# Up products 352 wide, with 32 tokens' inner values gathered early and written into the gate matrix as weights

## The chip, the core and the metric

The kernel runs on one core of a Trainium2 chip. The measure is the device time of one execution in microseconds. A core has five engines with instruction streams of their own: TensorE (PE in the profile, with its weight loads as PEld), VectorE (DVE), ScalarE (ACT), GpSimd (POOL) and SyncE (SP). Each of them works in the order of its own stream; they wait for one another by semaphores. DMAs are issued from the streams of SP, ACT and POOL.

## The reference, cut to what matters

A trunk of two layers over 512 tokens, 1024 wide. In each layer three causal mixers (attention, a short convolution, gated linear attention) are followed by a PEER channel mixer: a product-key lookup chooses, for each token, 8 heads x 16 of 16384 experts, each of them one row of u and one of v.

```python
def peer(xn, w_q, keys1, keys2, u, v):
    ...
    s1 = jnp.einsum('thd,nd->thn', q[:, :, 0], keys1).astype(jnp.float32)
    s2 = jnp.einsum('thd,nd->thn', q[:, :, 1], keys2).astype(jnp.float32)
    v1, i1 = lax.top_k(s1, PEER_TOPK)
    v2, i2 = lax.top_k(s2, PEER_TOPK)
    cand = (v1[..., :, None] + v2[..., None, :]).reshape(T, PEER_HEADS, PEER_TOPK * PEER_TOPK)
    sc, ci = lax.top_k(cand, PEER_TOPK)
    ...
    experts = (e1 * PEER_NKEYS + e2).reshape(T, hk)
    gates = jax.nn.softmax(sc, axis=-1).reshape(T, hk).astype(xn.dtype)
    ...
    def block(args):
        xb, eb, gb = args
        ub = jnp.take(u, eb, axis=0)
        hb = jax.nn.gelu(jnp.einsum('tkd,td->tk', ub, xb), approximate=False)
        vb = jnp.take(v, eb, axis=0)
        return jnp.einsum('tk,tkd->td', gb * hb, vb)
```

So for a token the output is the sum over its 128 chosen experts of gate x gelu(u row . x) x v row.

## The kernel before

**Two ways to the same sum.** For the first TD = 368 tokens PEER is computed densely, over all 16384 experts in 128 chunks of 128. `hidden` forms the inner values of a chunk (expert by token) as the up product of u and x, with GELU by ACT on the way out of PSUM (tile psh to tile ht). A gate matrix G, which is zero where a token has not chosen an expert, is multiplied in (`weigh`), and `accumulate` forms the down product with v into six PSUM banks (pv), 384 tokens by 1024. The last 128 tokens (block 3 of 4) and the 16 that remain of block 2 (tokens 368 to 383) go by gathering: an indirect DMA on POOL's queue fetches for each of the 128 partitions the row of one chosen expert, a DVE operation forms the inner product with x (`inner`, with accumulation along the row) or adds the weighted row of v to a sum (`outer`, into yacc).

**Three bf16-like parts.** Every large product is done in three matmuls (`mm3`) from a high and a low part of each operand; ACT makes the high part (a cast), DVE the low part (a subtraction). So each chunk of u, of v and of the weighted inner values costs an ACT and a DVE operation.

**The stages of the PEER part of a layer.** First the queries and the best keys of each head (`best`). Then the *up stage*: NPRE = 72 chunks, whose inner values are stored to memory (H), and three more; beside them DVE works at the routing (`routing`): for each block of 128 tokens `route` finds the 16 best of the candidates of each head, with their expert indices and gates, and `gate_matrix` builds G for 16 tokens at a time. For that it makes one-hot matrices of both halves of the expert index (oha, ohb) on DVE, multiplies one of them by the gate's high and low parts in fp16 (ohh, ohl), and PE multiplies 128x128 one-hots (psg) whose sums ACT copies out and stores. Then the *mixed stage*: 56 chunks in which an up product (24 matmuls, 368 columns) and a down product (18 matmuls, 512 columns) take turns. Then the *down stage*: 72 chunks of down products alone, with inner values that come back from H. The last three chunks' down products are prepared ahead (`ahead_v`, `ahead_hi`, `ahead_lo`) and stand at the end, one block of tokens at a time, with the next layer's norm between them.

**What sets the order.** The program is written in order; instructions marked `pin` stay in that order on their engine, the others are placed by a scheduler between them. Two generators run beside the chunks. `routing` is paced by DVE_STEP: it gives back the DVE time that it thinks it used, and gets 2.72 us of it a chunk. `gathered`, the row gathers, is paced by `tick` and RATE: 0.8 rows a chunk in the up stage (once the routing of block 3 is done), 3.3 in the mixed and 1.12 in the down stage. ROUTE_AT = 1 sets the routing of block 3 behind that of block 0.

**The 16 tokens between.** `route` of block 2 stores their experts and gates to memory (xidx, xgat); in the mixed stage, between the v rows of block 3, `spread` loads them so that the 16 tokens x 128 experts lie as 128 partitions x 16 (with the token's x repeated, tile xg), gathers 16 rows of u, then 16 of v, and a matmul with a placing matrix (psx) adds the eight partial sums of a token together and puts them at the tokens' rows.

**Buffers.** Four split chunks of u (tags uwa, uwb; NUW), five gathered rows (seven once the routing has closed), four raw v chunks, two tiles of G.

Of the kernel before, what the change touches and what calls it, by code (L numbers as in the profile page):

```python
# [19 lines left out]
P = 128  # L20
# [10 lines left out]
TD = 368  # L31
# [6 lines left out]
NPRE = 72  # L38
# [11 lines left out]
RATE = (0.8, 3.3, 1.12)  # L50
DVE_STEP = 2.72
ROUTE_AT = 1
# [20 lines left out]
class K:  # L73
# [18 lines left out]
    def setup(self):  # L92
# [10 lines left out]
        self.xidx = self.dr.tile([NX, P], I32, tag="xidx", name="xidx")  # L103
        self.xgat = self.dr.tile([NX, P], F32, tag="xgat", name="xgat")
# [623 lines left out]
    def peer(self, L, xh, xl, rest):  # L728
        nc, tc, ins = self.nc, self.tc, self.ins
        G = self.dr.tile([NCH // GE, P, TD // TBAT, GE * TBAT], F32, tag="G", name="G")  # L730
        H = self.dr.tile([NPRE, P, TD], F32, tag="H", name="H")
        with ExitStack() as pc:
# [9 lines left out]
            def new_h():  # L742
                if len(hts) < NHT:
                    hts.insert(0, self.up.tile([P, TW], F32, name=f"ht{len(hts)}", bufs=1))
                    nc.gpsimd.memset(hts[0][:, TD:TW], 0.0)
                else:
                    hts.insert(0, hts.pop())
# [70 lines left out]
            for j in range(NQ):  # L818
# [4 lines left out]
                if j == 3:  # L823
                    pin(nc.sync.dma_start(xg, ins["norm_ffn"][L:L + 1, :].partition_broadcast(P)))
# [12 lines left out]
                if j == 4:  # L837
                    nc.vector.scalar_tensor_tensor(xg, self.x[:, 3], self.rs3, xg, op0=OP.mult, op1=OP.mult)
# [33 lines left out]
            def spread():  # L872
                dma = nc.gpsimd.dma_start
                for _ in range(8):
                    yield False
                for i in range(NX):
                    dma(xg[i * XS:(i + 1) * XS], self.xrows[i:i + 1, :].partition_broadcast(XS))
                dma(xix, self.xidx.rearrange("i (s k) -> (i s) k", k=XR))
                dma(gat[:, 0:XR], self.xgat.rearrange("i (s k) -> (i s) k", k=XR))
                for _ in range(8):  # L880
                    yield False
                for k in range(XR):
                    inner(xix[:, k:k + 1], hd[:, k:k + 1])
                    yield True
                nc.scalar.activation(hd[:, 0:XR], hd[:, 0:XR], AF.Gelu)
                nc.vector.tensor_tensor(hd[:, 0:XR], hd[:, 0:XR], gat[:, 0:XR], op=OP.mult)
                for _ in range(8):
                    yield False
                dma(gat, ins["c_place"])
                for k in range(XR):  # L890
                    outer(xix[:, k:k + 1], hd[:, k:k + 1], xg, k == 0)
                    yield True
                for half in range(2):
# [468 lines left out]
```

## Time and profile before

| | |
|---|---|
| median of 3 runs | 2927.74 us (2927.54 to 2932.99) |
| the profiled execution, its own time | 2929.99 us |
| its span, first to last instruction | 2928.2 us |
| mean granted clock of TensorE | 0.999 |
| PE busy / weight loads busy | 2898.9 us / 2576.4 us |
| DVE / ACT / POOL busy | 2448.1 / 1254.0 / 858.8 us |
| moved by DMA | 788.65 MB, mean 269 GB/s |

The profile shows one execution. A row of a group gives the line, the engine, the operation, the tile written and those read, the count, the busy time, the mean of one in ns, and the engine's idle time ahead of it with what ended it. A row of the timeline gives the start and the length in us; in brackets the idle time ahead of it. A row of stretches gives, for a window in us, its length and then the busy time of the engines in the order of its heading. Matmuls overlap: each shows longer than the distance to the next one.

### The profile page before, as it was taken

The page shows a single profiled execution, that of the slowest core. Times are in us where ns is not written, and L with a number is a line of the kernel's source. Part 1 is how long each engine was busy: PE and PEld are TensorE (multiplying, and loading weights), DVE is VectorE, ACT ScalarE, POOL GpSimd, SP SyncE. Part 2 cuts the span into 40 slices and gives each one's busy share as a digit, 9 for nine tenths or more (in the row PEclk, how much of TensorE's full clock was granted, in tenths as well). Part 3 has the DMA queues.
Part 4 walks back from the last instruction along what each step waited for, and adds up shares of the span by engine and source line. Part 5 has one row for each costly group of instructions (what it writes and reads, how often), then busy time and mean ns, then how long its engine had stood idle before and what let it go on. Part 6 is the DMA issues. An engine that isn't in the chain of part 4 may idle for free.

```text
span 2928.2 us, 44773 instructions
## 1 busy us (share of the span) xinstructions
PE 2898.9 (99%) x16206; PEld 2576.4 (88%) x16206; DVE 2448.1 (84%) x4828; ACT 1254.0 (43%) x1910; POOL 858.8 (29%) x735
## 2 busy tenths in 40 slices
PE   8999999999999999999999999999999999999998
PEld 7878899999999998788888788999999999988887
DVE  6675998996888898988966769999958888988888
ACT  6253355655333332333453533556653333323333
POOL 1200001221555665322112000012215556663221
PEclk9999999999999999999999999999999999999999
DMA  4322258999999999999633222689989999999995
GB/s 130 94 69 82 88 171 269 314 303 352 335 362 359 348 395 349 393 361 370 261 97 90 68 82 88 205 272 314 314 319 354 370 366 347 394 347 386 370 373 210
DMA packets 342334, 788.65 MB, mean 269 GB/s; under 512 B 32640, under 2 KB 189344, under 8 KB 338016
## 3 DMA queue, kind: packets, MB, share of 16 engines
q1 hardware_dynamic: 160624, 430.73, 40.8%
q0 software_dynamic: 86400, 306.56, 28.5%
q10 hardware_dynamic: 95088, 48.50, 5.5%
q8 instruction: 127, 2.08, 0.3%
q14 instruction: 95, 0.78, 0.1%
HBM read 704.64 MB, written 77.89 MB: 267 GB/s over the span
## 4 chain that ended last, share of the span: by engine, by line
PE 85%; DVE 6%; issue 3%; DMA 3%; ACT 2%; POOL 1%; SPq 0%; DVEq 0%; ACTq 0%; POOLq 0%
PE pv L85 10%; PE psh L86 10%; PE psh L84 10%; PE pv L86 10%; PE psh L85 10%; PE pv L84 10%; PE psp L86 2%; PE psp L85 2%; PE psp L84 2%; PE psq L84 2%; PE psq L85 2%; PE psq L86 2%; PE psg L1290 1%; PE psg L1291 1%; DMA row<-in_v_rows,idx 1%
## 5 line engine op out<-in xcount | busy, mean ns | idle before, releaser
L857 POOL DMA_INDIRECT row<-in_u_rows,idx x256 | 371.4, 1451 | 989.2 <-DVE idx L1243 457.7
L85 PE MATMUL pv<-vl,wh 128*128 128x512 f32 x1500 | 582.9, 391 | 0.4
L86 PE MATMUL pv<-vh,wl 128*128 128x512 f32 x1500 | 582.4, 391 | 0.0
L84 PE MATMUL pv<-vh,wh 128*128 128x512 f32 x1500 | 575.0, 390 | 0.0
L857 POOL DMA_INDIRECT row<-in_v_rows,idx x256 | 326.6, 1276 | 431.9 <-DVE yacc L870 343.3
L774 ACT ACTIVATE ht<-psh 128x368 f32<-128x368 f32 x256 | 122.5, 478 | 733.3 <-PE psh L86 716.9
L1001 DVE TENSOR_TENSOR vl<-vraw,vh 128x1024 fp32r<-128x1024 f32 x250 | 305.6, 1223 | 83.5 <-ACT vh L1006 73.5
L863 DVE SCALAR_TENSOR_TENSOR row<-row,xg 128x1024 f32<-128x1024 f32 x288 | 345.5, 1219 | 0.0
L84 PE MATMUL psh<-ahi,uwb 128*128 128x368 f32 x1024 | 340.4, 332 | 0.0
L84 PE MATMUL psh<-ahi,uwa 128*128 128x368 f32 x1024 | 339.9, 332 | 0.0
L86 PE MATMUL psh<-ahi,uwa 128*128 128x368 f32 x1024 | 339.5, 332 | 0.0
L86 PE MATMUL psh<-ahi,uwb 128*128 128x368 f32 x1024 | 339.4, 331 | 0.0
L85 PE MATMUL psh<-alo,uwb 128*128 128x368 f32 x1024 | 337.7, 330 | 0.0
L85 PE MATMUL psh<-alo,uwa 128*128 128x368 f32 x1024 | 337.5, 330 | 0.0
L870 DVE SCALAR_TENSOR_TENSOR yacc<-row,wk,yacc 128x1024 f32<-128x1024 f32 x254 | 325.1, 1280 | 11.4 <-DMA row<-in_v_rows,idx 10.2
L86 PEld LDWEIGHTS pv<-vh,wl 128*128 128x128 f32 x1500 | 281.1, 188 | 60.5 <-DVE wl L1001 1.5
L85 PEld LDWEIGHTS pv<-vl,wh 128*128 128x128 f32 x1500 | 280.9, 188 | 59.9 <-DVE vl L1001 2.9
L84 PEld LDWEIGHTS pv<-vh,wh 128*128 128x128 f32 x1500 | 281.5, 188 | 56.1 <-ACT wh L1014 0.5
L1014 ACT CAST wh<-ht 128x384 fp32r<-128x384 f32 x250 | 128.0, 512 | 444.4 <-DVE ht L1166 405.5
L1006 ACT CAST vh<-vraw 128x1024 fp32r<-128x1024 f32 x250 | 262.4, 1050 | 1.4 <-PE pv L85 1.4
L759 DVE TENSOR_TENSOR uwb<-uraw,uwb 128x1024 fp32r<-128x1024 f32 x144 | 175.9, 1221 | 103.7 <-ACT uwb L758 97.2
L759 DVE TENSOR_TENSOR uwa<-uraw,uwa 128x1024 fp32r<-128x1024 f32 x144 | 175.3, 1221 | 71.8 <-ACT uwa L758 68.6
(381 smaller groups left out, 5828.0 us busy)
## 6 DMA issues: line engine op xcount, KB each, us to landing
uraw<-in_peer_u SPq DMA_DIRECT2D x256, 512.0 KB
vraw<-in_v_rows SPq DMA_DIRECT2D x256, 512.0 KB
G<-stg ACTq DMA_DIRECT2D x46, 1024.0 KB
g<-G SPq DMA_DIRECT2D x32, 1472.0 KB
H<-ht SPq DMA_DIRECT2D x144, 184.0 KB
ht<-H SPq DMA_DIRECT2D x144, 184.0 KB
wraw<-in_w_in SPq DMA_DIRECT2D x84, 256.0 KB
uraw<-in_peer_w_q SPq DMA_DIRECT2D x32, 512.0 KB
```

Of the source, the lines that this page charges most:

```text
L84: mm(ps, ah, bh, start=first, stop=False)
L85: mm(ps, ah, bl, start=False, stop=False)
L86: return mm(ps, al, bh, start=False, stop=last)
L759: self.before, self.last = self.last, pin(nc.vector.tensor_tensor(lo, src, hi.bitcast(F32), op=OP.subtract))
L774: pin(nc.scalar.activation(hs[c][:, 0:TD], ps, AF.Gelu))
L857: nc.gpsimd.indirect_dma_start(out=r, out_offset=None, in_=ins[name], in_offset=bass.IndirectOffsetOnAxis(ap=at, axis=0))
L863: nc.vector.scalar_tensor_tensor(r, r, 1.0, xg, op0=OP.mult, op1=OP.mult, accum_out=out)
L870: nc.vector.scalar_tensor_tensor(acc, r, w, acc, op0=OP.mult, op1=OP.add)
L1001: self.last = pin(nc.vector.tensor_tensor(lo, src, hi.bitcast(F32), op=OP.subtract))
L1006: pin(nc.scalar.copy(vh[c], vs[c]))
L1014: pin(nc.scalar.copy(wh[c], hs[c]))
L1290: nc.tensor.matmul(ps[:, j], B[at], AH[at], start=True, stop=False)
```

## The change

TD goes from 368 to 352, so the up products of each chunk are 352 columns wide and 32 tokens (352 to 383, NX = 32) are left of block 2. Their v rows are no longer gathered. Their 32 x 128 inner values (as 128 partitions x 32) are computed by gathered u rows beside the routing, at the start of `gathered`; then they pass through GELU, four small DMAs put them back into the layout of the gates (hx), DVE multiplies gate by inner value (gx), PE transposes, and ACT and DVE cut the result into three bf16 parts (W). `gate_matrix` builds the last two blocks of 16 tokens from these parts, with three products of the one-hot and three matmuls a token; the third product overwrites oha. So G holds, in the 32 columns, the finished weights, and `weigh` copies these columns into ht instead of multiplying them. G is 24 blocks wide, not 23.

The order of the routing becomes block 2, block 0, block 1, the wait for the 32 gathered rows, the two last blocks of G, then `route` of block 3. The gathers of block 3 start when that is done (`ready`). Until then xg holds the rows of the 32 tokens, loaded from xrows on POOL's queue during the queries; after them the norm's gain is loaded into it, on POOL's queue too (before: on SP's). The pacing: NPRE 72 to 74, RATE (0.8, 3.3, 1.12) to (0.62, 3.3, 1.15), DVE_STEP 2.72 to 2.6. The placing matrix, psx, xidx and xgat go.

```diff
-TD = 368
+TD = 352
...
-NPRE = 72
+NPRE = 74
...
-RATE = (0.8, 3.3, 1.12)
-DVE_STEP = 2.72
-ROUTE_AT = 1
+RATE = (0.62, 3.3, 1.15)
+DVE_STEP = 2.6
...
                 if j == 3:
-                    pin(nc.sync.dma_start(xg, ins["norm_ffn"][L:L + 1, :].partition_broadcast(P)))
+                    for i in range(XS):
+                        nc.gpsimd.dma_start(xg[i * NX:(i + 1) * NX], self.xrows)
...
-            def spread():
...
             def gathered():
+                for k in range(XR):
+                    inner(xix[:, k:k + 1], hd[:, k:k + 1])
+                    yield
+                nc.gpsimd.dma_start(xg, ins["norm_ffn"][L:L + 1, :].partition_broadcast(P))
+                while not ready:
+                    yield 1
+                nc.vector.scalar_tensor_tensor(xg, self.x[:, 3], self.rs3, xg, op0=OP.mult, op1=OP.mult)
                 for k in range(P):
                     inner(idx[:, k:k + 1], hd[:, k:k + 1])
                     yield
...
             def routing():
...
+                for tb in (xb, *range(xb)):
+                    gt = rp.tile([P, P], F32, tag="gt", name="gt")
+                    extra = (xix, gx, L * NCH * P) if tb == xb else None
+                    yield from self.route(V12[tb], I12[tb], rp, gt, hk=(E1, E2, GH, GL), tb=tb, extra=extra)
...
+                while done < XR:
+                    yield 0.0
+                r0, t0 = P - NX, TD - xb * P
+                nc.scalar.activation(hd[:, 0:XR], hd[:, 0:XR], AF.Gelu)
+                hx = rp.tile([P, P], F32, tag="sv", name="hx")
+                for i in range(XS):
+                    nc.gpsimd.dma_start(hx[r0:P, i * XR:(i + 1) * XR], hd[i * NX:(i + 1) * NX, 0:XR])
+                yield 0.0
+                nc.vector.tensor_tensor(gx[r0:P], gx[r0:P], hx[r0:P], op=OP.mult)
+                tr = self.psC.tile([P, P], F32, tag="c", name="rtr3")
+                pin(nc.tensor.transpose(tr, gx, self.ident))
+                W = [lp.tile([P, w], BF16, name=f"W{i}") for i, w in enumerate((NX, NX, 2 * NX))]
...
+                for bt in range(TD // TBAT, TW // TBAT):
+                    yield from self.gate_matrix(bt, E1, E2, W, G, hp, w0=TD)
+                yield from self.route(V12[3], I12[3], rp, gat, idx=idx, base=L * NCH * P)
+                ready = True
...
     def weigh(self, h, g, c):
...
+        gv = g[:, :, c % GE * TBAT:c % GE * TBAT + TBAT]
+        n = TD // TBAT
+        self.tc.keep_in_program_order(self.nc.vector.tensor_tensor(hv[:, 0:n], hv[:, 0:n], gv[:, 0:n], op=OP.mult))
+        self.tc.keep_in_program_order(self.nc.vector.tensor_copy(hv[:, n:], gv[:, n:]))
...
+            As = [hp.tile([P, ng, P, 2], kind, tag=n, name=n) for n in ("ohh", "ohl")] + [A] * (len(parts) - 2)
+            for a, w in zip(As, parts):
+                nc.vector.tensor_tensor(a, A, tok(w, t0 - w0), op=OP.mult)
...
+                        for a in As:
+                            nc.tensor.matmul(ps[:, j], B[at], a[at], start=a is As[0], stop=a is As[-1])
```

**Where instructions move.** POOL's queue, first layer, from the start of the row gathers. Before:

```order
L857 DMA row<-in_u_rows,idx 128x1024 x26
L1254 DMA xgat<-gt 16x128
L857 DMA row<-in_u_rows,idx 128x1024
L1253 DMA xidx<-xi_6687 16x128
L857 DMA row<-in_u_rows,idx 128x1024 x101
L857 DMA row<-in_v_rows,idx 128x1024 x7
L877 DMA xg<-xrows 8x1024
L857 DMA row<-in_v_rows,idx 128x1024 x2
L877 DMA xg<-xrows 8x1024 x15
L878 DMA hd<-xidx 128x16
L879 DMA gat<-xgat 128x16
```

The same place now (hd<-xi brings the 32 tokens' expert indices, hx<-hd their inner values):

```order
L821 DMA xg<-xrows 32x1024 x4
L1258 DMA hd<-xi 32x32 x4
L852 DMA row<-in_u_rows,hd 128x1024 x32
L873 DMA xg<-in_norm_ffn 128x1024
L934 DMA hx<-hd 32x32 x4
L852 DMA row<-in_u_rows,idx 128x1024 x128
L852 DMA row<-in_v_rows,idx 128x1024 x128
```

The 32 rows stand ahead of all of block 3's, and nothing stands between block 3's rows of v any more.

DVE in the up stage, near the end of the routing, where the inner values come back (uwa, uwb are the low parts of the split chunks of u; L858 is the last of the 32 inner products). There is no such place before; now:

```order
L858 SCALAR_TENSOR_TENSOR row,hd<-row,xg 128x1024
L1283 TENSOR_TENSOR oha<-iota_410,E_3662 128x2048
L755 TENSOR_TENSOR uwa<-uraw,uwa 128x1024
L1284 TENSOR_TENSOR ohb<-iota_410,E_3663 128x2048
L1287 TENSOR_TENSOR ohh<-oha,GH 128x2048
L1287 TENSOR_TENSOR ohl<-oha,GL 128x2048
L755 TENSOR_TENSOR uwb<-uraw,uwb 128x1024
L936 TENSOR_TENSOR gx<-gx,hx 32x128
L1283 TENSOR_TENSOR oha<-iota_410,E_3662 128x2048
L755 TENSOR_TENSOR uwb<-uraw,uwb 128x1024
```

Six operations lie between the last inner product and the product that waits for hx, and a split of u stands right behind it. After the two last blocks of G follows the whole of block 3's `route`, which before had lain between the blocks 0 and 1.

DVE at the end of the first layer's PEER part, from the next to last vl on (sll is the low part of the next layer's first weights). Before:

```order
L1001 TENSOR_TENSOR vl<-vraw,vh 128x1024
L1001 TENSOR_TENSOR wl<-ht_3896,wh 128x384
L1166 TENSOR_TENSOR ht_3930<-ht_3930,g 128x368
L870 SCALAR_TENSOR_TENSOR yacc<-row,wk,yacc 128x1024
L90 TENSOR_TENSOR sll<-first,slh 128x512
L1001 TENSOR_TENSOR vl<-vraw,vh 128x1024
L1001 TENSOR_TENSOR wl<-ht_3930,wh 128x384
L1101 TENSOR_TENSOR x<-x,yacc 128x1024
```

Now, from the last product with G on:

```order
L1168 TENSOR_TENSOR ht_3792<-ht_3792,g 128x352
L1169 COPY ht_3792<-g 128x32
L865 SCALAR_TENSOR_TENSOR yacc<-row,wk,yacc 128x1024
L89 TENSOR_TENSOR sll<-first,slh 128x512
L1001 TENSOR_TENSOR vl<-vraw,vh 128x1024
L1001 TENSOR_TENSOR wl<-ht_3792,wh 128x384
L865 SCALAR_TENSOR_TENSOR yacc<-row,wk,yacc 128x1024
L89 TENSOR_TENSOR sll<-first,slh 128x512
L865 SCALAR_TENSOR_TENSOR yacc<-row,wk,yacc 128x1024
L89 TENSOR_TENSOR sll<-first,slh 128x512
L865 SCALAR_TENSOR_TENSOR yacc<-row,wk,yacc 128x1024
L89 TENSOR_TENSOR sll<-first,slh 128x512
```

One more yacc row and then the addition of yacc to x follow. Four rows of yacc have moved behind the last wl, and each product with G has a copy behind it.

More of the change, by code (lines that the diff above doesn't have):

```diff
@@ L870, in outer, with gathered @@
                     nc.vector.scalar_tensor_tensor(acc, r, w, acc, op0=OP.mult, op1=OP.add)
-            def spread():
[L873 to L881, printed above, removed]
+            ready = False
+            def gathered():
                 for k in range(XR):
                     inner(xix[:, k:k + 1], hd[:, k:k + 1])
[L884 to L893, printed above, removed]
-                    n = slice(half * 512, half * 512 + 512)
-                    ps = self.psB.tile([P, 512], F32, tag="b", name="psx")
-                    nc.tensor.matmul(ps, gat, xg[:, n], start=True, stop=True)
-                    xs = self.x[96:P, NB - 1, n]
-                    nc.vector.tensor_tensor(xs, xs, ps[96:P], op=OP.add)
-            def gathered():
+                    yield
[3 more added lines that the diff above has]
+                nc.vector.scalar_tensor_tensor(xg, self.x[:, 3], self.rs3, xg, op0=OP.mult, op1=OP.mult)
                 for k in range(P):
@@ L909, in gathered @@
                     yield
-                    if next(others, False):
-                        yield
             side = gathered()
@@ L920, in tick @@
                 with tc.issue_after(self.last.ins):
-                    while done < want and next(side, 0) is None:
+                    while done < want:
+                        w = next(side, 0)
+                        if w is not None:
+                            want = done
+                            break
                         done += 1
@@ L939, in routing @@
             def routing():
-                for tb in range(TB):
-                    if tb == ROUTE_AT:
-                        yield from self.route(V12[3], I12[3], rp, gat, idx=idx, base=L * NCH * P)
+                nonlocal ready
+                xb, nb = NB - 1, P // TBAT
+                gx = rp.tile([P, P], F32, name="gx")
+                for tb in (xb, *range(xb)):
+                    gt = rp.tile([P, P], F32, tag="gt", name="gt")
+                    extra = (xix, gx, L * NCH * P) if tb == xb else None
+                    yield from self.route(V12[tb], I12[tb], rp, gt, hk=(E1, E2, GH, GL), tb=tb, extra=extra)
+                    if tb == xb:
@@ L943, in routing @@
                         yield None
[L944 to L947 removed]
                     for bt in range(min(P, TD - tb * P) // TBAT):
[L949 removed]
+                        yield from self.gate_matrix(tb * nb + bt, E1, E2, (GH, GL), G, hp, first=(tb, bt) == (xb, 0))
@@ new lines, in routing @@
+                pin(nc.tensor.transpose(tr, gx, self.ident))
+                W = [lp.tile([P, w], BF16, name=f"W{i}") for i, w in enumerate((NX, NX, 2 * NX))]
+                rest = rp.tile([P, NX], F32, tag="bi", name="rest")
+                nc.scalar.copy(W[0], tr[:, t0:P])
+                nc.vector.tensor_tensor(rest, tr[:, t0:P], W[0], op=OP.subtract)
+                nc.vector.tensor_copy(W[1], rest)
+                nc.vector.tensor_tensor(W[2][:, 0:NX], rest, W[1], op=OP.subtract)
+                yield 0.6
```

70 lines of the change are left out of this document (28 added, 42 removed).

## The prediction

> **What bounds the kernel now.** I read the page first, then the chain of work that ended last, then the busy time of each engine by stage, and last the instructions in order of time on the engine that carries the chain.
>
> ```profile
> PE 2898.9 (99%) x16206; PEld 2576.4 (88%) x16206; DVE 2448.1 (84%) x4828; ACT 1254.0 (43%) x1910; POOL 858.8 (29%) x735
> ...
> PE 85%; DVE 6%; issue 3%; DMA 3%; ACT 2%; POOL 1%; SPq 0%; DVEq 0%; ACTq 0%; POOLq 0%
> ```
>
> PE is busy for 99% of the span, but its spans overlap, so this alone does not say that it is the limit. The second line says more: 85% of the chain is PE. The three stages that the change touches, in the first layer (the second layer repeats them), are the up stage with the routing beside it, the mixed stage (up and down products in turn) and the down stage:
>
> ```profile
> core 0: us, PE busy (x) PEld busy (x) DVE busy (x) ACT busy (x) POOL busy (x), PEclk, DMA share, GB/s
> 376.50:729.00 352.50, 352.38 (x2568) 348.75 (x2568) 314.95 (x653) 210.25 (x269) 62.72 (x43) 1.00 0.86 290
> 729.00:1002.00 273.00, 273.00 (x1402) 247.84 (x1401) 228.87 (x332) 93.11 (x135) 152.58 (x120) 1.00 0.92 344
> 1180.00:1447.00 267.00, 267.00 (x1174) 219.76 (x1173) 234.83 (x282) 100.65 (x138) 75.30 (x68) 1.00 0.97 367
> ```
>
> PE has no gap worth naming in any of the three; DVE stands at 89%, 84% and 88%. So a nanosecond off a matmul counts in full as long as DVE keeps its cover, and the question is what a matmul's step is. I take it from start to start:
>
> ```profile
> 269.75 0.28 PE L84 MATMUL psq<-ahi,uwa 128*128 128x256 f32 x1
> ...
> 273.89 0.28 PE L86 MATMUL psq<-ahi,uwa 128*128 128x256 f32 x1
> ...
> 334.26 0.40 PE L85 MATMUL psq<-alo,uwa 128*128 128x512 f32 x1
> ...
> 335.89 0.40 PE L86 MATMUL psq<-ahi,uwb 128*128 128x512 f32 x1
> ...
> 799.92 0.33 PE L84 MATMUL psh<-ahi,uwa 128*128 128x368 f32 x1
> ...
> 801.94 0.33 PE L84 MATMUL psh<-ahi,uwa 128*128 128x368 f32 x1
> ...
> 1299.80 0.39 PE L84 MATMUL pv<-vh,wh 128*128 128x512 f32 x1
> ...
> 1301.84 0.39 PE L84 MATMUL pv<-vh,wh 128*128 128x512 f32 x1
> ```
>
> The first pair is 35 steps apart (118.3 ns each at 256 columns), the second 7 (232.9 ns at 512), the third 12 (168.3 ns at 368), the fourth 9 (226.7 ns at 512, other tiles). The first three use the same kind of weight tile and the same moving tile, and they lie on one line: 0.446 ns a column from 256 to 368, 0.449 from 368 to 512.
>
> **The change, part by part.**
>
> Up products, 368 to 352 columns. 16 columns at 0.447 ns are 7.15 ns; 2 layers x 128 chunks x 24 matmuls are 6144; together -43.9 us, all on PE.
>
> Gate matrix. It has 24 blocks of 16 tokens a layer where it had 23, and one fewer of the old kind (22 and 2): the last two take three matmuls a token. That is 736 to 800 matmuls a layer, 128 more in all.
>
> ```profile
> 0.00:2929.00 2929.00, 92.57 (x1472) 177.41 (x184) 1.00 0.75 269
> ...
> 1192.12 1.72 PE psx L896 x4
> ...
> 408.23 0.27 PE L1256 MATMUL rtr<-ident,ex 128*128 128x128 f32 x1
> ```
>
> The first row is the stretch of the whole span for the tile psg: 62.9 ns a matmul, so +8.1 us. The scatter product psx goes, 1.72 us of the chain a layer: -3.4 us. One more transpose a layer like the third row: at most +0.5, I take +0.3.
>
> Gathers. Before, 16 tokens had 16 row gathers of U and 16 of V a layer; now 32 tokens have 32 of U and none of V. The count (288) is the same, only 32 now must end inside the up stage (before, 34 of another kind lay there). No cost by itself.
>
> DVE in the up stage.
>
> ```profile
> L759 DVE TENSOR_TENSOR uwb<-uraw,uwb 128x1024 fp32r<-128x1024 f32 x37 | 45.1, 1220 | 20.7 <-ACT uwb L758 20.5
> L863 DVE SCALAR_TENSOR_TENSOR row<-row,xg 128x1024 f32<-128x1024 f32 x34 | 41.4, 1218 | 0.0
> L1278 DVE TENSOR_TENSOR oha<-iota,E 128x2048 f16<-128x2048 f16 x23 | 28.1, 1220 | 0.1
> ...
> L1293 ACT ACTIVATE stg<-psg 128x512 f32<-128x512 f32 x92 | 88.5, 1127 | 4.7 <-DMA G<-stg 4.7
> ```
>
> Added: two chunks' splits (2 x 1.22), one block of four one-hot operations more (4.9), a third product in two blocks (2.4), some 1.5 us of small ones; two gathers fewer (-2.4): 315 becomes about 324. The stage itself: 352.5 - 75 x 24 x 7.15 ns (12.9) + 2 chunks of 24 x 161 ns (7.7) + 64 psg (4.0) = 351.3. So DVE goes from 89% to 92%, ACT from 60% to 62% (four evictions of 1.13 and two chunks). I cost it at nothing: PE is covered by four split tiles of U, two chunks of work. If that cover goes, DVE's surplus comes through one for one.
>
> The wait for the inner values. The 32 columns of inner values pass through GELU, four small DMAs on POOL's queue, a product on DVE, a transpose on PE and a copy on ACT before the last two blocks. DVE stops in its order at that product, and the U splits stand behind it. Nearest rows, a like transfer by issue time and in the chain of waits:
>
> ```profile
> L877 POOL DMA_DIRECT2D xg<-xrows x16: 505/510/568, 973.3 to 990.3; - x16
> ...
> 986.83 5.78 DMA xg<-xrows
> ```
>
> Ahead of them on POOL's queue now stands the load of the norm's gain into xg, which was SP's (0.51 more, and 512 KB in front of them on the way), behind them the first gathers by idx, which have the rest of the stage to land. The other DMAs that move or go (the rows of the 32 tokens, their indices and gates) lie in stages where POOL is busy 63 of 352 us or less. Four issues of 0.51 and a landing of 5.8 are 7.8 us, with the gain 8.3, less the six or seven operations that DVE does in between (last inner product, one-hots and splits, 1.14 to 1.22 each: about 7). That leaves 0 to 8 us a layer on DVE, most of it under PE's lead; I take 1 a layer, +2. The gain end is zero: nothing that was waited for goes here.
>
> The down stage: a copy joins the chain between DVE and ACT, since the columns of the 32 tokens are copied from G, not multiplied.
>
> ```profile
> 1301.94 0.53 DVE L1166 TENSOR_TENSOR ht<-ht,g 128x368 f32<-128x368 f32 x1
> 1302.39 1.28 DVE L870 SCALAR_TENSOR_TENSOR yacc<-row,wk,yacc 128x1024 f32<-128x1024 f32 x1
> 1304.14 1.23 DVE L1001 TENSOR_TENSOR vl<-vraw,vh 128x1024 fp32r<-128x1024 f32 x1 [0.47 <-ACT vh L1006]
> 1305.28 0.55 DVE L1001 TENSOR_TENSOR wl<-ht,wh 128x384 fp32r<-128x384 f32 x1
> 1305.75 0.54 DVE L1166 TENSOR_TENSOR ht<-ht,g 128x368 f32<-128x368 f32 x1
> ...
> 1302.63 0.51 ACT L1014 CAST wh<-ht 128x384 fp32r<-128x384 f32 x1 [3.10 <-DVE ht L1166]
> 1303.06 1.05 ACT L1006 CAST vh<-vraw 128x1024 fp32r<-128x1024 f32 x1
> ...
> 1433.51 0.54 DVE L1166 TENSOR_TENSOR ht<-ht,g 128x368 f32<-128x368 f32 x1
> 1433.96 2.60 DVE L870 SCALAR_TENSOR_TENSOR yacc<-row,wk,yacc 128x1024 f32<-128x1024 f32 x2
> ...
> L1206 DVE COPY d<-i 128x16 f16<-128x16 f16 x4 | 0.7, 164 | 0.0
> ...
> L1182 DVE TENSOR_TENSOR cand<-V 128x32 f32<-128x32 f32 x4 | 0.7, 186 | 0.0
> L1238 DVE TENSOR_TENSOR gt<-gt,zs 128x128 f32<-128x128 f32 x3 | 0.9, 285 | 0.0
> ```
>
> The product with G lets ACT make wh, then vh, then DVE vl, wl and the next product: 1301.94 to 1305.75, a loop of 3.81 us against PE's 18 x 226.7 ns = 4.08. A chunk with two gathers takes 1.2 more on DVE, where half a microsecond of waiting is filled first: about 4.5. With 1.12 gathers a chunk the mean is 3.81 x 0.88 + 4.5 x 0.12 = 3.89. The copy of 128x32 costs 0.164 (the smallest copy) to 0.285 us (a 128x128 operation); the form nearest in size has 0.186. In order, an operation starts some 0.08 before the one ahead has ended (1.28 long, and the next 1.20 later), so about 0.11 of it counts: 3.92 x 0.85 + 4.6 x 0.15 = 4.02 at the new rate of 1.15. PE still has 0.06 of cover: 0. By the upper price the mean is 4.2, 0.11 over PE's, on 70 chunks and two layers +16 us. The mixed stage has more room: a chunk there is 24 x 161 + 18 x 226.7 ns = 7.95 us, DVE 84% of the former 8.12 plus the copy, 88%.
>
> The end of a layer. Row gathers now end later: four of the products on yacc stand behind the last wl, where before none did.
>
> ```profile
> 1447.20 1.28 DVE L870 SCALAR_TENSOR_TENSOR yacc<-row,wk,yacc 128x1024 f32<-128x1024 f32 x1
> ...
> 1450.13 0.55 DVE L1001 TENSOR_TENSOR wl<-ht,wh 128x384 fp32r<-128x384 f32 x1
> 1450.60 1.22 DVE L1101 TENSOR_TENSOR x<-x,yacc 128x1024 f32<-128x1024 f32 x1
> ...
> 1479.34 1.29 DVE L223 TENSOR_TENSOR alo<-psn,ahi 128x512 fp32r<-128x512 f32 x2 [1.43 <-ACT ahi L222]
> ```
>
> From the last wl to the last alo DVE works almost without a break, and the next layer's first products wait for alo. Four products of 1.2 us there make the norms 4.8 us later in the first layer: +5, between 0 (PE's remaining pv products cover it) and +10 (the last gathers land late as well). In the last layer the same work ends under three groups of pv: +0.
>
> G is read 24 blocks wide, not 23, H 352 columns, not 368: +8 and -8 KB a chunk, nothing.
>
> Sum: -43.9 + 8.1 - 3.4 + 0.3 + 2 + 5 = -31.9 us. The profiled execution took 2929.99 us (span 2928.2), 2.25 above the median of the runs shown, so 2898.1 in its terms and **2896** at the median.
>
> **The rivals.** *The weight loads set the step.* In the up stage the weight loads are busy 348.75 of 352.5 us, more than 98%. If they set the 168.3 ns, fewer columns give nothing, and the additions stay: 2896 + 43.9 = 2940, slower. It decides if the step at 352 columns stays above 167 ns. Against it: at 256 columns the same load of a 128x128 f32 tile passes every 118.3 ns. The Trainium skill (Perfetto Trace Analysis, Identifying the Most-Contended Engine) counsels to judge TensorE's headroom by the busy share of LDWEIGHTS, not of matmuls, and read so it speaks for this rival. The step at 256 columns disagrees with it here: that share counts loads that overlap. 6%.
>
> *DVE's loop outgrows PE in the down stage.* The copy at its upper price: 2896 + 16 = 2912, and a few more if the up stage also loses its cover. For it speaks the slack of only 0.06 us. 13%.
>
> *The inner values come late.* The DMAs meet a full queue (DMA share 0.86), DVE stands 8 us or more and PE runs out of split tiles, or the last gathers end the layer: 10 to 12 us a layer, 2918 with both. 10%.
>
> *368 columns are an odd width.* At pv's 226.7 / 512 = 0.443 ns a column, 368 should take 163; if the rest belongs to the width and 352 takes 156, the gain is 76 us and the time 2864. Against it: psq shows the same surplus at 256 and 512. 5%.
>
> **How the numbers follow.** The forecast has 64%, with its own range 2887 to 2911 (layer end 0 to 10, wait 0 to 6 a layer, a column 0.443 to 0.46 ns). What is left, 2%, is a slower end of no named kind. The range 2880 to 2922 takes in the forecast, the loop and most of the late inner values, and leaves out the odd width and the weight loads. Within 0.2%, 5.9 us of the median (2922 to 2934), which is about what a measurement of this kernel can tell from no change, lie the worse ends of the loop and the wait: 6%. Slower: 8%. Faster: 86%.
>
> **What would show it.** Right: psh steps of about 161 ns from start to start; PE without gaps in the three stages; a mixed chunk of 7.95 us; 1600 psg matmuls; no psx; DVE near 92% in the up stage. Wrong: psh still at 168; PE waiting for vl or wl in the down stage with a DVE loop above 4.08; a wait of DVE for hx longer than 3 us with PE's gap behind it; a gap of more than 6 us on PE where the first layer ends.

## The result and the profile after

| | before | after |
|---|---|---|
| median (6 runs each) | 2928.10 us (2927.18 to 2932.99) | 2912.78 us (2910.18 to 2914.78) |
| ratio after to before | | 0.9944 (95%: 0.9931 to 0.9957) |
| the profiled execution, its own time / span | 2929.99 / 2928.2 us | 2913.61 / 2911.8 us |

The kernel is faster by 15.3 us (0.5%). The forecast was 31.9 us, so a little under half of it came. The range 2880 to 2922 holds the time; the forecast's own range, 2887 to 2911, does not. From the page of the changed kernel, the busy times and the chain of work that ended last:

```profile
PE 2862.0 (98%) x16328; PEld 2532.0 (87%) x16328; DVE 2476.5 (85%) x5130; ACT 1261.4 (43%) x1921; POOL 855.5 (29%) x709
...
PE 68%; issue 12%; DVE 7%; POOL 7%; DMA 3%; ACT 2%; SPq 0%; POOLq 0%; ACTq 0%; DVEq 0%
```

PE is busy for 36.9 us less, but the span is only 16.4 us shorter: PE idles 50 us where it idled 29. In the chain PE falls from 85% to 68%, and POOL has 7% of it where it had 1%. The three stages, columns as in the prediction (PE, PEld, DVE, ACT, POOL busy, clock, DMA share, GB/s):

```profile
376.00:735.00 359.00, 351.07 (x2686) 346.94 (x2686) 320.13 (x663) 215.52 (x278) 58.81 (x48) 0.99 0.86 284
735.00:1002.00 267.00, 266.38 (x1401) 240.71 (x1400) 238.14 (x385) 99.17 (x139) 151.75 (x105) 1.00 0.96 366
1134.00:1460.00 326.00, 324.17 (x1423) 264.00 (x1422) 293.12 (x432) 119.09 (x167) 104.23 (x88) 1.00 0.93 351
```

In these stretches PE lacks 0.6 us of the mixed and 1.8 us of the down stage, each in pieces of at most 1.4 us. In the up stage PE lacks 8 us of 359, where before it lacked 0.1 of 352.5. The same by the clock, from the first and last matmul of psh and pv in the trace (us, first / second layer):

| stretch | before | after | forecast's terms |
|---|---|---|---|
| up: first psh to first pv (76, now 78 chunks) | 354.2 / 353.9 | 360.0 / 360.2 | 354.0 / 353.7 |
| mixed: to the last psh (52, now 50 chunks) | 424.7 / 424.7 | 399.3 / 399.5 | 398.0 / 398.0 |
| down: to the last pv | 318.0 / 313.6 | 325.9 / 323.4 | 326.2 / 321.8 |
| last pv to the next layer's first psh / to the end | 356.1 / 8.2 | 359.0 / 9.4 | 361.1 / 8.2 |

The forecast's column puts each of its terms at its place (up: 354.2 - 12.9 for the width + 7.7 for two chunks + 4.0 for psg + 1 for the wait). It counted one chunk fewer in the up stage than the trace shows, 0.2 us. Of the 15.5 us that are missing in the span, 12.5 lie in the two up stages. The step itself is better than forecast. Two rows of PE in order of time, in the up stage:

```profile
724.99 0.32 PE L83 MATMUL psh<-ahi,uwb 128*128 128x352 f32 x1
...
731.39 0.32 PE L84 MATMUL psh<-alo,uwa 128*128 128x352 f32 x1
```

They are 40 steps apart, 160.0 ns each. The mean over all steps without a gap is 160.0 in the up and 160.25 ns in the mixed stage; before it was 168.9 and 168.8. So the width alone is worth 8.7 ns x 6144 = 53 us, not 43.9. A psg matmul takes 57.4 ns from start to start inside its groups where nothing holds it up: 128 of them are 7.3 us, a little less than the 8.1 of the forecast.

What PE lacks is one gap per layer of some 7 us and a few of 1 to 3. The large one, on PE, then on DVE, and last the stretch of all engines behind it:

```profile
423.58 0.32 PE L83 MATMUL psh<-ahi,uwb 128*128 128x352 f32 x1
429.44 0.61 PE L1297 MATMUL psg<-ohh,ohb 128*128 128x128 f16 x4 [5.54 <-DVE ohh L1287]
...
417.05 1.22 DVE L1287 TENSOR_TENSOR ohl<-oha,GL 128x2048 f16<-128x2048 f16 x1
422.75 1.22 DVE L858 SCALAR_TENSOR_TENSOR row<-row,xg 128x1024 f32<-128x1024 f32 x1 [4.49 <-DMA row<-in_u_rows,hd]
...
424.74 1.23 DVE L858 SCALAR_TENSOR_TENSOR row<-row,xg 128x1024 f32<-128x1024 f32 x1 [0.75 <-DMA row<-in_u_rows,hd]
...
428.16 1.22 DVE L1287 TENSOR_TENSOR ohh<-oha,GH 128x2048 f16<-128x2048 f16 x1
...
430.00:433.50 3.50, 3.50 (x24) 3.25 (x24) 3.50 (x4) 1.25 (x2) 0.00 (x0) 0.50 1.00 364
```

DVE stands in its order at the first of the 32 inner products until its row has landed. The one-hots of the second gate block stand behind it, the psg products that need them stand at the head of PE's order, and PE stops although psh products wait behind them. The Trainium skill (TensorE: Matmul & The Clock Gate, Part 2, Step-by-step: what each phase is for) states that matmuls stay in program order and only weight loads are pulled ahead. The trace agrees: psh started at 429.80, right behind the first four psg products, without a wait of its own.

The stop itself is 5.5 us long. Behind it, until 433.7 us, the granted clock is 0.50, and PE's steps are nearly twice as long: 293 ns for psh instead of 160, 107 for psg instead of 57. That costs 2.0 us more in the first layer and 1.8 in the second, where the same happens at 1868 us. In the sums below it is counted in part.

### The profile page after: what moved, and what is told of

Its sections match the earlier page's. It is cut to its first block, busy times and chain, and to the rows that moved or that the text cites. A ratio compares the mean times of both kernels' runs of the same rounds, so it can differ in the third digit from the quotient of the medians.

```text
span 2911.8 us, 45325 instructions
## 1 busy us (share of the span) xinstructions
PE 2862.0 (98%) x16328; PEld 2532.0 (87%) x16328; DVE 2476.5 (85%) x5130; ACT 1261.4 (43%) x1921; POOL 855.5 (29%) x709
## 4 chain that ended last, share of the span: by engine, by line
PE 68%; issue 12%; DVE 7%; POOL 7%; DMA 3%; ACT 2%; SPq 0%; POOLq 0%; ACTq 0%; DVEq 0%
PE pv L84 9%; PE pv L85 9%; PE pv L83 8%; POOL row L852 7%; PE psh L83 6%; PE psh L84 6%; PE psh L85 6%; PE psp L84 3%; PE psp L85 3%; PE psp L83 3%; PE psg L1297 2%; PE psq L83 2%; PE psq L84 2%; PE psq L85 2%; PE pss L789 1%
## 5 line engine op out<-in xcount | busy, mean ns | idle before, releaser
L852 POOL DMA_INDIRECT row<-in_u_rows,idx x256 | 365.1, 1426 | 407.1 <-DVE row L858 261.2
L852 POOL DMA_INDIRECT row<-in_v_rows,idx x256 | 332.5, 1299 | 446.7 <-DVE yacc L865 413.8
L770 ACT ACTIVATE ht<-psh 128x352 f32<-128x352 f32 x256 | 119.1, 465 | 657.4 <-PE psh L85 635.6
L858 DVE SCALAR_TENSOR_TENSOR row<-row,xg 128x1024 f32<-128x1024 f32 x320 | 382.4, 1219 | 10.6 <-DMA row<-in_u_rows,hd 10.6
L83 PE MATMUL psh<-ahi,uwa 128*128 128x352 f32 x1024 | 334.6, 327 | 0.0
L83 PE MATMUL psh<-ahi,uwb 128*128 128x352 f32 x1024 | 334.5, 327 | 0.0
L84 PE MATMUL psh<-alo,uwb 128*128 128x352 f32 x1024 | 331.4, 324 | 0.0
L84 PE MATMUL psh<-alo,uwa 128*128 128x352 f32 x1024 | 330.6, 323 | 0.0
L85 PE MATMUL psh<-ahi,uwb 128*128 128x352 f32 x1024 | 327.7, 320 | 0.0
L85 PE MATMUL psh<-ahi,uwa 128*128 128x352 f32 x1024 | 326.8, 319 | 0.0
```

The costliest lines, as they stand in the source:

```text
L83: mm(ps, ah, bh, start=first, stop=False)
L84: mm(ps, ah, bl, start=False, stop=False)
L85: return mm(ps, al, bh, start=False, stop=last)
L770: pin(nc.scalar.activation(hs[c][:, 0:TD], ps, AF.Gelu))
L852: nc.gpsimd.indirect_dma_start(out=r, out_offset=None, in_=ins[name], in_offset=bass.IndirectOffsetOnAxis(ap=at, axis=0))
L858: nc.vector.scalar_tensor_tensor(r, r, 1.0, xg, op0=OP.mult, op1=OP.mult, accum_out=out)
```

## The experiments

Two theories to begin with. *W*: this one wait, which the forecast did not see, costs what is missing. *L*: DVE was already at its limit beside the routing, and the shorter chunks of PE cannot be cashed there. From the stretches 400 to 640 us of before and of after:

```profile
400.00:640.00 240.00, 239.88 (x1772) 237.15 (x1771) 228.26 (x468) 145.58 (x188) 43.83 (x30) 1.00 0.86 286
...
400.00:640.00 240.00, 232.07 (x1819) 228.64 (x1819) 228.50 (x398) 150.43 (x193) 48.12 (x36) 0.99 0.91 300
```

In both DVE works 228 of 240 us, 95%; the 89% of the whole stage is a mean with its idle ends. PE's gaps below are start-to-start excesses in the up stage, summed from the timeline together with the wait at the first pv, and good to about 1 us: in the changed kernel 10.7 us in the first layer (7.0 at 424 to 431, 2.6 at 600, 1.0 at 735) and 11.3 in the second.

### The first row asked for later

```diff
-            spent, live = 0.0, False
+            spent, live = 0.0, NPRE
...
-                if live and c < NPRE - 2:
+                if live <= c < NPRE - 2:
...
-                        live = True
+                        live = c + 3
```

> The only edit: the first of the 32 gathered rows is asked for three chunks (some 12 us) later, so that other one-hot operations and a split stand in DVE's order ahead of the first inner product. Theory W (the wait): in the changed kernel DVE stands 4.5 + 0.75 us at the first two of the 32 inner products, whose rows have not landed, and the gate products of the second block stand at the head of PE's order and wait for that DVE: a gap of some 7 us on PE a layer. Then this edit gives both gaps back: up stage 360 to 353 us, 2912.8 - 14 = 2899. Rival L (the load): DVE is 89% busy in the up stage and its work does not fit between the shorter chunks; then the gap only moves to a later place and the time stays within 4 us of 2912.8.

Measured: 2917.10 us (ratio 0.996, 0.9947 to 0.9974), 4 above the changed kernel; the intervals of the two overlap, so these 4 us are not sure, but the forecast 2899 is clearly missed. Whom PE waited for in the up stage, and one wait of DVE there (us, times, longest):

```profile
PE psg L1297 <- ACT stg L1299: 3.1, 5, 1.6
PE psg L1297 <- DVE ohh L1287: 2.1, 3, 1.8
PE rtr L938 <- DVE gx L936: 1.6, 1, 1.6
...
DVE gx L936 <- DMA hx<-hd: 7.4, 1, 7.4
```

The wait for the row is gone and the gap of 7 us with it (1.2 are left at 422). But the gaps are 10.9 and 13.4 us a layer, at 456, 498, 600 and 664 us now; in the first layer none is longer than 2 us, and the clock stays at 1.00. W falls as a sufficient cause. The rows end later, and DVE waits 7.4 us for hx instead of 3.4, with PE's transpose behind it.

### G and v loaded a chunk earlier

```diff
-                if c == NPRE - 1:
+                if c == NPRE - 2:
                     load_v(order[0])
-                if c == NPRE:
+                if c == NPRE - 1:
                     load_g(order[0])
                     load_v(order[1])
```

> The only edit: the first G tile and the first two v chunks are loaded one chunk earlier, ahead of the mixed stage. Theory: the first pv products wait 1.0 us in the first and 1.8 us in the second layer for vl, whose chain begins with the product that waits 2.1 us for the G tile; loaded earlier both go: 2912.8 - 2 to -3 = 2910. Rival: the transfers there only change places with the u chunks, since the DMA queues are 0.86 to 0.96 busy: between 0 and +2.

Measured: 2919.93 us (0.9963 to 0.9984), 7 above the changed kernel. The rival was right, and more so: pv no longer waits, but ACT stands before a cast of u, and psh has gaps of 3.3 and 4.2 us at 731 and 2181.

```profile
716.89 0.51 SPq L962 DMA_DIRECT2D g<-G  x1
...
733.02 1.04 ACT L754 CAST uwb<-uraw 128x1024 fp32r<-128x1024 f32 x1 [8.85 <-DMA uraw<-in_peer_u]
```

The transfer of 1.5 MB goes ahead of a chunk of u that is needed sooner.

### The copy three times

```diff
+        self.tc.keep_in_program_order(self.nc.vector.tensor_copy(hv[:, n:], gv[:, n:]))
+        self.tc.keep_in_program_order(self.nc.vector.tensor_copy(hv[:, n:], gv[:, n:]))
```

> The copy of the 32 finished columns is done three times instead of once, with the same result: two more operations of 0.18 us behind each product with G, of which 0.09 each count in DVE's order. If DVE's loop is close under PE's 4.08 us a chunk, as forecast: with one gather 3.89 becomes 4.07, with two 4.6 becomes 4.8, the mean at 1.15 gathers a chunk 4.18: +0.1 us x 72 chunks x 2 layers = +14, so 2927, with pv gaps before vl and wl all through the down stage. If the loop has more room than that (DVE can run ahead by its two vl tiles): 0 to +3.

Measured: 3292.85 us, 380 above. Far off both values, because the edit did more than it said. DVE in the down stage of the changed kernel, then of this one:

```profile
1298.25 0.52 DVE L1168 TENSOR_TENSOR ht<-ht,g 128x352 f32<-128x352 f32 x1
1298.68 0.17 DVE L1169 COPY ht<-g 128x32 f32<-128x32 f32 x1
1298.77 1.28 DVE L865 SCALAR_TENSOR_TENSOR yacc<-row,wk,yacc 128x1024 f32<-128x1024 f32 x1
1300.53 1.22 DVE L1001 TENSOR_TENSOR vl<-vraw,vh 128x1024 fp32r<-128x1024 f32 x1 [0.48 <-ACT vh L1006]
1301.67 0.55 DVE L1001 TENSOR_TENSOR wl<-ht,wh 128x384 fp32r<-128x384 f32 x1
1302.14 0.52 DVE L1168 TENSOR_TENSOR ht<-ht,g 128x352 f32<-128x352 f32 x1
```
```profile
1502.51 0.52 DVE L1168 TENSOR_TENSOR ht<-ht,g 128x352 f32<-128x352 f32 x1
1502.94 0.17 DVE L1169 COPY ht<-g 128x32 f32<-128x32 f32 x1
1503.03 1.28 DVE L865 SCALAR_TENSOR_TENSOR yacc<-row,wk,yacc 128x1024 f32<-128x1024 f32 x1
1504.22 0.17 DVE L1170 COPY ht<-g 128x32 f32<-128x32 f32 x1
1504.43 0.18 DVE L1171 COPY ht<-g 128x32 f32<-128x32 f32 x1
...
1507.88 0.52 DVE L1168 TENSOR_TENSOR ht<-ht,g 128x352 f32<-128x352 f32 x1
```

The three copies write the same columns one after another, and the scheduler put the gather between them. So the gather's 1.2 us, which otherwise lie beside ACT's casts, stand ahead of wh. The loop is 5.37 us instead of 3.89, over PE's 4.1, and the down stage takes 438 us instead of 326, the mixed stage 475.4 instead of 399.3. Two things follow. The unchanged kernel's loop is 3.89 us with its copy and a gather, as forecast (3.92), and PE covers it. And a loop that does outgrow PE comes through in full. What 0.2 us more would cost was not measured.

### The new way at the old width

```diff
-TD = 352
+TD = 368
...
+                nc.vector.memset(hx[96:P], 0.0)
...
-                nc.vector.tensor_tensor(gx[r0:P], gx[r0:P], hx[r0:P], op=OP.mult)
+                nc.vector.tensor_tensor(gx[96:P], gx[96:P], hx[96:P], op=OP.mult)
```

> The new way with the old width: up products 368 columns wide, 16 tokens left (16 rows gathered early, one block of the gate matrix in three parts); the product with the inner values covers rows 96 to 127, of which the unused ones are zero. Width: 6144 matmuls x 7.15 ns = +43.9 us, 96 gate matmuls fewer x 62.9 ns = -6.0. Theory W: the wait for the first row does not depend on the width or on DVE's load, so its gaps stay: 2912.8 + 37.9 = 2950.7. Rival L: 16 inner products fewer and 0.17 us more a chunk give DVE room and the gaps close: 2934 to 2941.

Measured: 2955.92 us (ratio 1.0096, 1.008 to 1.0111). The expectation counted 96 matmuls fewer; the pages show 16296 against 16328, 32 fewer, so W's value should have read 2954.7. That the time lies so near it is chance: with the 53 us that the width is worth by the steps, W would give 2964, and the 8 us below it are about what the closed gaps are worth. The gap behind the first row stays (5.4 us of PE in the first layer) and the gaps at 600 and 735 are gone, so each theory holds for its own gap. Without the width the new way is 28 us slower than before; the width brings 43 on top of it, out of the 51 that PE's steps are worth (53 less 2 for the 32 matmuls).

### The old way at the new width

```diff
-TD = 368
+TD = 352
```

> The kernel before with one number changed: up products 352 wide, the 32 tokens that are left go the old way (32 row gathers of u and 32 of v beside the mixed stage, the placing matrix), pacing as before. PE: 6144 x 8.6 ns (the step measured at 352 against 368 columns) = -53 us. DVE: 32 gathered rows a layer more, 38 us of operations in stages where DVE is 84 to 90% busy. If the pacing leaves them to the end of the layer, +32 to +38 a layer: 2928 - 53 + 70 = 2945, slower than before; if they fit beside PE, as little as 2880, and then the new way of the 32 tokens would have been needless.

Measured: 2990.57 us (ratio 1.0219, 1.0205 to 1.0233), 63 slower than before. The width's gain is there (160.1 ns a step) and the rows do not fit. DVE behind the end of the first layer, and the stretch in which PE waits:

```profile
1459.21 27.70 DVE L870 SCALAR_TENSOR_TENSOR yacc<-row,wk,yacc 128x1024 f32<-128x1024 f32 x21
...
1450.00:1520.00 70.00, 30.08 (x197) 27.08 (x196) 54.75 (x83) 14.22 (x26) 27.19 (x35) 0.71 0.58 202
```

PE has one gap of 38 us there. Its up stage has the routing of the kernel before, less one block of G, and its gathers (the first row at 494 us), and only the width is new; yet PE has gaps there, 9.3 us in all (4.1 at 621, 2.1 at 406, 1.6 at 535), at the transposes and the first gate products behind a route, where before it had 0.4. So shorter chunks alone open gaps in the up stage, with no early row to wait for. That speaks for L, and not for W.

### Half of the early sums left out

```diff
-            def inner(at, out):
+            def inner(at, out, n=D):
...
-                    inner(xix[:, k:k + 1], hd[:, k:k + 1])
+                    inner(xix[:, k:k + 1], hd[:, k:k + 1], D // 2)
```

(`inner` then works on the first n columns; the second variant also has live = c + 3)

> The 32 early inner products are formed over the first 512 of the 1024 columns only, so half of these sums is left out; the rows are still gathered whole. DVE has about 0.55 x 32 = 18 us a layer less to do in the routing part of the up stage; order and waits stay. Theory L (the load: between 400 and 640 us DVE is 95% busy, and what it is given there no longer fits beside PE, whose chunks have become shorter): the later gaps, some 4 us a layer, close, those 7 us behind the first row's wait stay: 2912.8 - 8 = 2905. Theory W (only the wait counts, the later start had a cost of its own): within 3 of 2912.8.

> Both edits: the first row three chunks later, and half of each of the 32 early sums left out. Theory L: the later start alone only moved the gaps, because DVE had no time to spare; with 18 us a layer less on DVE nothing takes their place, and all 11 us a layer come back: 2912.8 - 22 = 2891. Theory W with a cost of the later start (the inner values reach the gate matrix later, a wait of 7.4 us for them instead of 3.4, whatever DVE's load): the cost stays, 2913 to 2917.

Measured: 2910.70 us (0.9927 to 0.9954) with the first row at its old place and 2910.32 (0.9922 to 0.9949) with it three chunks later. Against the same kernels with the whole sums, 2912.78 and 2917.10, 18 us a layer less on DVE bring 2 us, which the overlapping intervals do not tell from nothing, and 7 us. By the times W is nearer: 2910.70 lies in its interval, 2910.32 between the two. By the places it is L: the gap at 600 us closes in both, the one behind the first row stays in the first of them (6.7 us). But the second keeps 8.0 us of gaps in the first layer of its profiled execution (2904.42, the fastest of its five), 2.9 of them at 456. L as a mere sum of DVE's work is too strong as well. Whom PE waited for in the second one, whom ACT waited for, and ACT at 456 us:

```profile
PE psg L1297 <- ACT stg L1299: 3.4, 7, 1.4
PE psg L1297 <- DVE ohh L1287: 1.1, 2, 1.0
...
ACT uwa L754 <- DMA uraw<-in_peer_u: 7.1, 6, 4.2
ACT stg L1299 <- DMA G<-stg: 5.5, 1, 5.5
...
455.71 1.05 ACT L754 CAST uwa<-uraw 128x1024 fp32r<-128x1024 f32 x1 [4.18 <-DMA uraw<-in_peer_u]
456.67 3.73 ACT L1299 ACTIVATE stg<-psg 128x512 f32<-128x512 f32 x4
```

ACT evicts psg into stg, whose buffer is free only when an earlier block of G has been stored: that wait ends at 437.7 us, and PE's gap of 2 us at 439 to 443 stands behind it. At 456 it is another wait: ACT stands at the cast of a chunk of u that has not landed, and the evictions of psg stand behind that cast.

### More chunks in the up stage

```diff
-NPRE = 74
-RATE = (0.62, 3.3, 1.15)
-DVE_STEP = 2.6
+NPRE = 78
+RATE = (0.6, 3.5, 1.15)
+DVE_STEP = 2.46
```

(the second variant has RATE[0] = 0.62 and live = c + 2)

> Nothing left out: four more chunks (78) in the up stage beside the same routing, DVE_STEP 2.6 to 2.46, RATE (0.6, 3.5, 1.15). The up stage gets 4 x 3.84 = 15 us more of PE work for 5 us more of DVE's. Theory L: the later gaps close (4 us a layer), the first wait stays: 2905, if the mixed stage, where DVE rises from 89 to 92%, keeps PE covered. Rival: the mixed stage with 3.5 rows a chunk or the end of the layer takes it back: 2913 to 2925.

> As the 78 chunks, with the first row two chunks later. Theory L: with room for DVE in the up stage the first wait can be moved without its coming back elsewhere: gaps of the up stage from 10.7 to under 3 us a layer, 2912.8 - 16 = 2897. Rival (the later start costs by itself, or the mixed stage is full): 2910 or more.

Measured: 2931.38 us (ratio 1.0007, 0.9998 to 1.0016) and 2929.96 (1.0001, 0.9992 to 1.001). The first layer's gaps of the up stage shrink from 10.7 to 6.6 us, as expected. The rival takes it back and more: the mixed stage hands DVE's arrears to the down stage, whose first four chunks have gaps of 8.0 us, and the down stages are 7.7 and 6.7 us longer than their four more chunks explain. The mixed stages, too, are 5 us longer each than their four fewer chunks of 7.97 us explain. Waits of the first layer's down stage:

```profile
PEld pv L84 <- DVE vl L1001: 12.2, 13, 3.3
PE pv L84 <- DVE vl L1001: 7.7, 5, 2.9
```

DVE has little room in any of the three stages; work that is moved between them finds it taken.

### Gathers beside the gate blocks only

```diff
+                    lull = True
                     yield from self.route(V12[tb], I12[tb], rp, gt, hk=(E1, E2, GH, GL), tb=tb, extra=extra)
+                    lull = False
...
-                if live and c < NPRE - 2:
-                    tick(RATE[0])
+                if live <= c < NPRE - 2:
+                    tick(0 if lull else RATE[0])
```

(with live = c + 3 and RATE[0] = 0.86)

> As the later start (three chunks), and the 32 early rows are asked for only beside the blocks of the gate matrix (0.86 a chunk), none beside a block's route. Theory P (the pacing): a chunk costs PE 24 x 160 ns = 3.84 us where a route runs and about 1 us more where gate products stand between; DVE is asked for a split of 1.14, 2.6 of routing and 0.62 x 1.2 of gathers, 4.5 us, so it falls behind beside every route, and PE waits at the first gate products behind it (at 424, 498 and 600 us). Without gathers there 3.74 us are asked for, and the gaps close: up-stage gaps from 11 to 13 us a layer with the later start alone to about 4, 2917 - 14 = 2903. Rival (the sum of DVE's work is what doesn't fit): the gaps move again, 2911 to 2917.

Measured: 2917.33 us (0.9945 to 0.9972), as the later start alone. The theory was right on its places: no gap is left at 498, 0.4 us at 597 (1.6 at the same place of the second layer). It was wrong on the sum: 10.7 us of gaps again in the first layer, at 422 (1.2), 456 (3.8), 670 (3.2), 685 (0.8), 735 (1.4) above all, and some 14 in the second. Whom PE waited for:

```profile
PE psg L1299 <- ACT stg L1301: 3.8, 5, 2.3
PE rtr L940 <- DVE gx L938: 2.7, 1, 2.7
PE psg L1299 <- DVE ohh L1289: 0.8, 2, 0.6
```

The second row is the inner values again, which come back late because the rows end late.

### The route of block 3 ahead of the last gate blocks

```diff
-                while done < XR:
-                    yield 0.0
-                ...
-                    yield from self.gate_matrix(bt, E1, E2, W, G, hp, w0=TD)
-                yield from self.route(V12[3], I12[3], rp, gat, idx=idx, base=L * NCH * P)
-                ready = True
+                for w in self.route(V12[3], I12[3], rp, gat, idx=idx, base=L * NCH * P):
+                    if not sent and done >= XR:
+                        send()          # GELU and the four small DMAs to hx
+                        sent = True
+                    yield w
+                ready = True
+                ...
+                    yield from self.gate_matrix(bt, E1, E2, W, G, hp, w0=TD)
```

(on top of the kernel above, RATE[0] = 0.84; the second variant also has RATE[1:] = 3.2, 1.22)

> As the kernel with gathers beside the gate blocks only (0.84 a chunk), and the route of block 3 stands ahead of the two last blocks of the gate matrix, with the four small DMAs of the inner values issued inside it, so that their landing lies beside that route. Theory: the wait of 7 us for hx goes as well, and three rows of block 3 come into the up stage: 2 us a layer below the kernel without this order, 2899 if that one takes 2903; without the pacing's gain 2910.

> As the kernel with route of block 3 ahead of the last gate blocks, with 3.2 rows a chunk in the mixed and 1.22 in the down stage instead of 3.3 and 1.15. Theory: the gaps of 2 to 3 us a layer behind the switch from the mixed to the down stage are DVE's backlog out of the mixed stage and shrink: 2 to 4 us below. Rival: the down stage's loop (3.89 us with one gather, about 4.75 with two, mean 4.08 at 1.22) loses its last cover: 0 to +10.

Measured: **2904.34 us** (ratio 0.9916, 0.9903 to 0.993), 8.4 below the changed kernel and 13 below the kernel without this order, and 2911.26 (0.9925 to 0.9952) with the other rates. From the page of the first:

```profile
PE 2859.0 (99%) x16328; PEld 2528.4 (87%) x16328; DVE 2478.0 (85%) x5130; ACT 1262.5 (44%) x1922; POOL 866.6 (30%) x709
...
PE 86%; DVE 5%; DMA 4%; ACT 3%; issue 1%; SPq 0%; DVEq 0%; ACTq 0%
```

The theory had put it 4 us below the kernel without this order, so the order was worth more than was thought. DVE does as much as in the changed kernel and does it at better places: no wait for hx is left, the up stage takes 358.4 and 358.3 us (with six psh matmuls more in it than in the changed kernel), the stretch between the layers 356.5 instead of 359.0, and PE is 86% of the chain again. The rates taken the other way cost 7 us: the down stages are 2.3 and 2.6 us longer, as the rival said, and the second layer's up stage is 3.7 us longer, which neither theory explains. The first is the fastest kernel of this study. Its up stages still lie some 8 us over what its steps add up to (first layer 350.5: 354.2 - 16.1 for the width + 7.7 for two chunks + 3.7 for psg + 1.0 for the six psh). 6.4 and 7.6 us of that are visible gaps, at 456 us among others.

## Why the prediction was right or wrong

**The gain's sign and place: right.** psh falls to 160 ns a step, PE has only small gaps in the mixed and down stages, psx is gone, 1600 psg are there, and a mixed chunk takes 7.97 us from start to start where 7.95 was forecast.

**The price of a column: mis-sized.** The step went from 168.8 to 160.1 ns, 0.54 ns a column, where the line through 256, 368 and 512 columns gave 0.447: -53 us, not -43.9. The 168.3 ns of the prediction came from rounded starts over 12 steps; the mean is 168.8, which changes the line by little. The point at 352 lies below the line, and no run shows why. The direction of the fourth rival was right, its size (76 us) was not. The rival of the weight loads is out: they are busy 346.94 of 359 us in the up stage, 97%, and the step fell all the same, so the rule of the Trainium skill (Perfetto Trace Analysis, Identifying the Most-Contended Engine) that judges TensorE's headroom by that share, read as this rival reads it, would have misled here.

**"I cost it at nothing: PE is covered by four split tiles of U": the step that failed.** It was read from a share of a whole stage, 89%, that had to rise to 92%. The amount of DVE's work was not too low: it rose by 5 us, 314.95 to 320.13, where 9 were forecast. Its place was overlooked. Beside the routing DVE had worked 228 of 240 us before, and the four tiles cover psh only: psg waits for DVE without any of them. The up stages came out 12.5 us over the forecast although their steps were 3 us a layer shorter than forecast. The runs take this apart into waits that replace one another: the first gathered row (7 us of PE a layer, gone with the later start), arrears behind a route (2.6 at 600, gone with half the sums and at 368 columns, 0.4 in the first layer with gathers beside gate blocks only), the inner values (nothing in the changed kernel, 1.8 to 3.2 when the rows end later, gone with block 3's route ahead). Without the first, and without the first and second, the time was 2917; only with all three away did it fall to 2904.

**The first row: not in the forecast.** It priced the way back of the inner values (0 to 8 us of DVE, 3.4 measured, no gap of PE behind it) and overlooked the way out: four small DMAs and a gather, from 410.37 to 422.75 us, with only six operations of DVE between. Nor did it have a price for the clock: behind the stop that follows, PE ran at half of it for 4 us.

**The down stage: right.** 3.89 us with a gather, no gap above 1.4 us. That the time lies near the 2912 of the rival of that place is chance; the table shows that stage where the forecast had it.

**The end of the layer: too dear.** +5 forecast, +2.9 measured between the layers, and 1.2 at the end where nothing was forecast. The last rows on DVE:

```profile
1446.88 1.27 DVE L865 SCALAR_TENSOR_TENSOR yacc<-row,wk,yacc 128x1024 f32<-128x1024 f32 x1
1448.08 0.68 DVE L1136 TENSOR_TENSOR x<-x,pv 128x512 f32<-128x512 f32 x1
1448.67 1.21 DVE L1101 TENSOR_TENSOR x<-x,yacc 128x1024 f32<-128x1024 f32 x1
```

**Each half alone.** Width without the new way 2991, new way without the width 2956, both 2913, neither 2928: each half alone is slower, and the forecast's sum of independent terms could not have said so of the pacing.

**Open.** The gap at 456 us stands in the first layer of four of the five kernels whose first row is asked for three chunks later, and not in the changed kernel. The traces of these four agree on the wait: ACT stands 4.2 to 4.7 us at the cast of a chunk of u, with the evictions of psg behind it; SP had issued that chunk only at about 450 us, when a split on DVE had freed its buffer. Some 13 us earlier ACT had waited 4.8 to 5.9 us for a store of G, and such stores land later beside gathers (below). That the gathers cause the late store, and the late store the late chunk, was not tested.

## What to carry to other kernels

Judge an engine's cover in the stretch where it is asked for most, not over a stage: a mean of 89% hid 95%. When the bounding engine gets faster, every engine that was level with it becomes the bound, and a wait that is removed uncovers the next; taken away one at a time they gave nothing, or 2 us that cannot be told from nothing, and only the kernel with three of them away gained clearly. A first use that follows a chain of small transfers wants more work of its engine ahead of it than the chain is long, and a consumer that stands at the head of an in-order engine spreads any such wait to work that was ready.

## What the runs showed of the hardware that was not expected

Between 368 and 352 columns a step fell by 8.7 ns, 0.54 ns a column, more than the 0.447 of the line through 256, 368 and 512.

The granted clock fell behind a stop of PE. After 5.5 us without a matmul it was 0.50 from 430 to 433.5 us (the changed kernel), after 3.9 us in the old way at 352 columns it was 0.50 from 625 to 628 us, and the steps were longer until it was back. So a stop of that length cost more than the time that PE stood still.

The stores of G take longer beside row gathers. Issues from 400 to 480 us with their size and the median from issue to landing in us, of the old way at 352 columns (no row is gathered in that stretch), then of the fastest kernel:

```profile
G<-stg ACTq DMA_DIRECT2D x8, 1024.0 KB, 4.8
```
```profile
G<-stg ACTq DMA_DIRECT2D x6, 1024.0 KB, 10.8
row<-in_u_rows,hd POOLq DMA_INDIRECT x11, 8.1
```

With 11 gathered rows between them the stores land in 10.8 us instead of 4.8, at a DMA share of 0.92 instead of 0.78. Two stretches are compared here; no run changed the gathers alone.
